# Mixer B's query weights in smaller tiles, a fourth raw weight buffer, other hands for the first down sums, and a later norm

## The chip, the core and the metric

The kernel runs on one core of one Trainium2 chip. What is compared is the device time of one execution in microseconds (us), as the median of several runs. One run of each kernel is also profiled; every duration below comes from that profile or from the runs' times. Engines are named as in the profile: PE (TensorE matmuls), PEld (its weight loads), DVE (VectorE), ACT (ScalarE), POOL (GpSimd), SP (SyncE, which issues transfers here).

## The reference: what is computed

Two layers over 512 positions of width 1024, in float32. The parts that this case touches:

```
for l in range(2):
    h = rms_norm(x, norm_mix[l]);  z = h @ w_in[l]
    qa, ka, va, qi, ki, wi, cq, ckv, kr, ga, gb = split(z)
    # mixer A: index scores relu(qi.ki)*wi -> top 128 keys per query -> sparse attention
    y_a = sparse_indexed_attention(qa, ka, va, qi, ki, wi, rel_bias, 128)
    # mixer B: latent attention
    qb = rope(rms_norm(cq) @ b_w_uq[l])          # 384 -> 8 heads x 96
    k, v = split(rms_norm(ckv) @ b_w_ukv[l])     # 256 -> 8 heads x (64 + 64)
    y_b = latent_attention(rms_norm(qb), rms_norm([k, rope(kr)]), v)
    x = x + (sigmoid(ga)*(y_a @ w_proj_a[l]) + sigmoid(gb)*(y_b @ w_proj_b[l])) @ w_out[l]
    h = rms_norm(x, norm_ffn[l])
    val, gat = split(causal_dwconv(h @ w_up[l]))
    x = x + (silu(gat) * val) @ w_down[l]        # 2816 -> 1024
```

## The kernel before

Activations lie transposed, the 128 partitions holding features and the 512 columns the positions. Every float32 product is made of three matmuls of a narrower kind: each operand is split into a high part and a low part (high times high, high times low, low times high). So each weight tile passes through three stages, all in the class `Weights`: a load from HBM into a raw buffer `wr` (issued on SP, line 154), a cast into the high part `wh` (ACT, L171, or L189 for down tiles), and the low part `wl`. The low part is a DVE subtraction (L183, or L194 for down tiles), or, for the tiles named in `DL` (`gb`, `ga`, `uv`, `ug`, `kv`, `uq`), a negated copy on ACT (L199) onto which a transfer issued by POOL adds the raw tile (L200, "wl<-wr"). There are `WB[0]` = 3 raw buffers and `WB[1]` = 4 buffers each for high and low parts, all as wide as the widest tile, `W_COLS`. A raw buffer is free again when its tile's low part is made. `PLAN` lists the tiles in the order of use; `ahead()` runs at the end of each tile's matmuls, splits the tiles up to three ahead and issues the loads behind them.

A down tile ("dn", 512 loaded columns) is made into seven blocks by three operations (`sums`): L209 and L210 (128x128 subtractions) and L211 (a 128x256 addition). L211 is always on POOL; L210 is on POOL in the second FF part only (`SU2 = '12'`), L209 never.

The program runs: index-query tiles `qi`, index key tile `kiw`, latents `ckv` and `cq`, with the index scores (L319, L320 on PE, `rl` on ACT L983, `sc` on DVE L984) set between them; then mixer B (`kv` L815, `uq` L852, scores L1125 to L1127, softmax) between the `gb` gate tiles, while DVE works off the top-128 search in spare slots (MAX8, L996, and MATCH_REPLACE8, L1003); then mixer A, the merge, and the feed-forward stage in two parts, each with its up tiles `uv`, `ug` and then its down tiles. A helper, `later(n, f)`, puts work on an engine `n` ticks after the point where it is written, one tick per three matmuls; all queues run strictly in the order that results, so a waiting instruction holds everything behind it on its engine.

The norm at the head of a layer adds up squares on DVE (`sq`, L457) and then reduces them with four 1-column matmuls against `ones` (`finish`, L463). `LAG_F` and `LAG_G` say how many ticks later these are put, in layer 0 and in layer 1.

The query weights of mixer B are in one tile of 1152 columns per group of four heads (3 blocks of 384). Its nine matmuls per bank go block by block: high tile twice, low tile once.

## Time and profile before

| | us |
|---|---|
| median of 3 runs (1553.75 to 1557.57) | 1554.92 |
| the profiled execution | 1551.76 |
| its span | 1550.0 |
| PE busy / PEld busy in the span | 1532.2 / 1335.8 |
| DVE / ACT / POOL busy in the span | 1126.9 / 944.7 / 376.9 |

The span is the time between the first and the last instruction of the profiled execution; 1.76 us lie around it. PE's busy time counts matmuls whose ends are modelled, so a matmul behind a wait is shown somewhat long and the idle time ahead of it somewhat short. The granted clock of TensorE was 1.0 of full speed (2.4 GHz) throughout.

### The profile page before, as it was taken

To read this page: it belongs to the slowest core of one execution; us is meant where nothing else is said; L and a number is where in the kernel's file an instruction comes from. 1 tells how busy PE (TensorE), PEld (TensorE's weight loads), DVE (VectorE), ACT (ScalarE), POOL (GpSimd) and SP (SyncE) were. 2 spreads that over 40 slices of the span, in tenths; PEclk is the share of its full clock that TensorE was granted. 3 is DMA by queue.
4 is the path that set the end of the run, shared out by engine and by line. 5 is a ranking of instruction groups with operands and counts; after the bars stand their busy time and mean duration, and the time that the engine had idled before them with its cause. 6 is when DMAs were issued, how large, how long until landed. Compare 5 with 4: busy or idle time off the path is not lost.

```text
span 1550.0 us, 23962 instructions
## 1 busy us (share of the span) xinstructions
PE 1532.2 (99%) x8662; PEld 1335.8 (86%) x8662; DVE 1126.9 (73%) x2323; ACT 944.7 (61%) x1547; POOL 376.9 (24%) x550
## 2 busy tenths in 40 slices
PE   9999999999999999999999999999999999999998
PEld 7887999888888898889988889998888888988898
DVE  7799988666476683548879999886574857835487
ACT  6756677773567535764467576687635764366542
POOL 1233003300012241224602420124001113312254
PEclk9999999999999999999999999999999999999999
DMA  7573134733478437983455721346435883489733
GB/s 249 152 174 96 55 96 98 189 111 134 122 183 198 109 97 196 224 190 84 123 176 121 185 82 55 102 123 168 140 98 137 187 196 89 120 205 211 178 96 103
DMA packets 71687, 219.02 MB, mean 141 GB/s; under 512 B 8384, under 2 KB 8680, under 8 KB 71440
## 3 DMA queue, kind: packets, MB, share of 16 engines
q1 hardware_dynamic: 53248, 149.41, 31.0%
q0 software_dynamic: 17856, 65.28, 23.0%
q10 hardware_dynamic: 464, 2.79, 0.6%
q8 instruction: 68, 1.11, 0.3%
q14 instruction: 51, 0.42, 0.1%
HBM read 143.77 MB, written 6.84 MB: 97 GB/s over the span
## 4 chain that ended last, share of the span: by engine, by line
PE 74%; DVE 10%; DMA 3%; ACT 2%; issue 2%; POOL 1%; DVEq 0%; POOLq 0%; SPq 0%; ACTq 0%
PE D L519 35%; PE T L519 13%; PE D L542 7%; PE L L1381 4%; PE T L1381 3%; PE Y L1041 2%; PE T L1034 2%; PE D L1381 2%; DMA wr<-in_wd_dram 2%; PE Y L1381 2%; DVE wl L194 1%; PE L L519 1%; PE L L320 1%; PE L L319 1%; DMA wl<-wr 1%
## 5 line engine op out<-in xcount | busy, mean ns | idle before, releaser
L171 ACT CAST wh<-wr 128x1024 fp32r<-128x1024 f32 x202 | 211.8, 1050 | 172.6 <-PE D L519 63.2
L200 POOL DMA_DIRECT2D wl<-wr x124 | 107.3, 873 | 640.1 <-ACT wl L199 587.1
L519 PE MATMUL D<-hxh,wh 128*128 128x512 f32 (+1 forms) x448 | 176.8, 395 | 0.9 <-ACT sqc L634 0.9
L519 PE MATMUL D<-hxl,wh 128*128 128x512 f32 (+1 forms) x448 | 175.5, 392 | 0.0
L189 ACT CAST wh<-wr 128x896 fp32r<-128x896 f32 x88 | 82.7, 941 | 118.0 <-POOL wr L211 101.9
L199 ACT ACTIVATE wl<-wr 128x1024 fp32r<-128x1024 f32 x124 | 131.5, 1061 | 33.5 <-PE D L519 21.8
L211 POOL TENSOR_TENSOR wr<-wr 128x256 f32<-128x256 f32 x88 | 101.9, 1158 | 90.9 <-DVE wr L210 77.1
L1076 POOL TENSOR_TENSOR P<-M,sel 128x128 f32<-128x128 f32 (+1 forms) x64 | 54.3, 902 | 277.1 <-DMA M<-skewd 253.0
L519 PE MATMUL D<-hxh,wl 128*128 128x512 f32 (+1 forms) x448 | 120.4, 394 | 0.0
L194 DVE TENSOR_TENSOR wl<-wr,wh 128x896 fp32r<-128x896 f32 x88 | 104.5, 1187 | 13.5 <-ACT wh L189 12.3
L542 PE MATMUL D<-wh,hxh 128*128 128x256 f32 x384 | 114.0, 298 | 0.0
L542 PE MATMUL D<-wl,hxh 128*128 128x256 f32 x384 | 108.8, 284 | 0.0
L542 PE MATMUL D<-wh,hxl 128*128 128x256 f32 x384 | 108.3, 282 | 0.0
L183 DVE TENSOR_TENSOR wl<-wr,wh 128x1024 fp32r<-128x1024 f32 x78 | 97.3, 1251 | 8.2 <-ACT wh L171 6.6
L519 PE MATMUL D<-hrl,wh 128*128 128x512 f32 x256 | 99.6, 389 | 0.0
L519 PE MATMUL D<-hrh,wh 128*128 128x512 f32 x256 | 99.6, 389 | 0.0
L519 PE MATMUL T<-hrh,wh 128*128 128x512 f32 x256 | 99.6, 389 | 0.0
L519 PE MATMUL T<-hrl,wh 128*128 128x512 f32 x256 | 99.6, 389 | 0.0
L519 PEld LDWEIGHTS D<-hxh,wh 128*128 128x128 f32 x448 | 84.4, 188 | 14.3 <-ACT sqc L634 1.3
L519 PEld LDWEIGHTS D<-hxl,wh 128*128 128x128 f32 x448 | 84.4, 188 | 12.6
L519 PEld LDWEIGHTS D<-hxh,wl 128*128 128x128 f32 x448 | 81.1, 188 | 13.3
L299 DVE TENSOR_TENSOR ptl<-T,pth 128x512 fp32r<-128x512 f32 (+3 forms) x128 | 61.0, 485 | 21.4 <-ACT pth L298 20.3
(400 smaller groups left out, 4516.6 us busy)
## 6 DMA issues: line engine op xcount, KB each, us to landing
wr<-in_wd_dram SPq DMA_DIRECT2D x198, 512.0 KB, 3.9
wl<-wr POOLq DMA_DIRECT2D x120, 512.0 KB, 5.5
wr<-in_wd_dram SPq DMA_DIRECT2D x88, 256.0 KB, 2.7
x<-in_xT_dram SPq DMA_DIRECT2D x16, 256.0 KB, 5.1
M<-skewd SPq DMA_DIRECT2D x16, 256.0 KB, 4.0
skewd<-biasd ACTq DMA_DIRECT2D x1, 2560.0 KB, 13.9
wr<-in_wd_dram SPq DMA_DIRECT2D x4, 576.0 KB, 4.2
wl<-wr POOLq DMA_DIRECT2D x4, 576.0 KB, 6.2
```

The costliest lines, as they stand in the source:

```text
L171: ins = self.nc.scalar.copy(h[:, :n], t[:, :n])
L183: eng.tensor_tensor(out=o[:, c], in0=t[:, c], in1=h[:, c].bitcast(F32), op=OP.subtract)
L189: self.nc.scalar.copy(h[:, :896], t[:, 128:1024])
L194: self.later(lag, lambda: self.nc.vector.tensor_tensor(out=o[:, :896], in0=t[:, 128:1024], in1=h[:, :896].bitcast(F32), op=OP.subtract))
L199: self.nc.scalar.activation(o, t, AF.Copy, scale=-1.0)
L200: self.nc.gpsimd.dma_start(o.bitcast(F32), t, accum_op=OP.add)
L211: g(2)(out=b[:, 6:8], in0=b[:, 0:3:2], in1=b[:, 3:6:2], op=OP.add)
L299: later(lag, lambda: V.tensor_tensor(out=o, in0=src, in1=h.bitcast(F32), op=OP.subtract))
L519: mm(p[:, t0:], lhsT=w, rhs=x[:, t0:], start=n == 0, stop=n == len(seq) - 1, skip_group_check=True)
L542: mm(pp[b][:, t, :], lhsT=x, rhs=w, start=n == 0 and half == 0 and t == 0, stop=n == 11 and half == 1, skip_group_check=True)
L1076: G.tensor_tensor(out=P[:, P0[i]:P0[i] + w], in0=M[:, 512 - w:512], in1=sel[:, SEL0[i]:SEL0[i] + w], op=OP.add)
L1381: mm(p, lhsT=w, rhs=x, start=b0, stop=b1, skip_group_check=True)
```

## The change

Three settings and two pieces of code differ. `LAG_F` and `LAG_G` go from 26 to 29 ticks. `WB[0]`, the number of raw buffers, goes from 3 to 4. Each `uq` tile of 1152 columns becomes two, of 768 and 384 columns, so `W_COLS` falls from 1152 to 1024 and all raw, high and low buffers become narrower; the nine matmuls of a bank now take the six products with high parts first and the three with low parts after. And in `sums`, a down tile whose fourth predecessor is not a down tile (the first four of each FF part) has all three operations on POOL.

```diff
-LAG_F = 26
+LAG_F = 29
-WB = [3, 4, 3]
+WB = [4, 4, 3]
-LAG_G = 26
+LAG_G = 29
@@ dense_plan
-    p += [("kv", 0, 1024), ("uq", 0, 1152)]
+    p += [("kv", 0, 1024), ("uq", 0, 768), ("uq", 1, 384)]
-    p += [("kv", 1, 1024), ("uq", 1, 1152)]
+    p += [("kv", 1, 1024), ("uq", 2, 768), ("uq", 3, 384)]
@@ Weights.sums
         su = SU2 if self.seq[i][1] % 11 >= FS // 2 else SUMS
+        if self.seq[i - WB[1]][0] != "dn":
+            su = "012"
@@ attn_b
-            h, o = W.get("uq", g)
+            tiles = [W.get("uq", 2 * g + i) for i in range(2)]
...
-                seq = ([(x, h, k) for k in range(3) for x in xs[k]] + [(xs[k][0], o, k) for k in range(3)] if "k" in LO
-                       else [q for k in range(3) for q in ((xs[k][0], h, k), (xs[k][1], h, k), (xs[k][0], o, k))])
-                for n, (x, w, k) in enumerate(seq):
-                    mm(p[:, 0:384], lhsT=x, rhs=w[:, k * 384:(k + 1) * 384], start=n == 0, stop=n == 8,
-                       skip_group_check=True)
+                seq = [(x, 0, k) for k in range(3) for x in xs[k]] + [(xs[k][0], 1, k) for k in range(3)]
+                for n, (x, part, k) in enumerate(seq):
+                    w = tiles[k // 2][part][:, k % 2 * 384:k % 2 * 384 + 384]
+                    mm(p[:, 0:384], lhsT=x, rhs=w, start=n == 0, stop=n == 8, skip_group_check=True)
@@ lay_out: the host lays the two pieces out one behind the other
```

The lines of the changed kernel below `sums` are one or two higher in number than before (L463 becomes L465, L519 becomes L521, L633 becomes L635).

What this does to the order on the engines, at three places. First, ACT in layer 0, behind the two casts of the index key (`kih`): `ckr` and `sqc` empty the first `ckv` bank of PE, `wn` is the copy from which the index weights are made, `wh` and `wl` belong to the next weight tile. Before:

```order
L571 CAST kih_481<-ki_479 64x512
L171 CAST wh_590<-wr_455 128x1024
L586 COPY wn_501<-T_496 128x160
L199 ACTIVATE wl_591<-wr_455 128x1024
L633 ACTIVATE ckr_528<-D_457,vec 128x512
L634 ACTIVATE sqc_529<-D_457 128x512
L983 ACTIVATE rl_547<-L_544,w_81_503 128x512
```

After:

```order
L573 CAST kih_492<-ki_490 64x512
L635 ACTIVATE ckr_504<-D_459,vec 128x512
L636 ACTIVATE sqc_505<-D_459 128x512
L588 COPY wn_523<-T_518 128x160
L171 CAST wh_574<-wr_396 128x1024
L984 ACTIVATE rl_558<-L_555,w_84_525 128x512
L199 ACTIVATE wl_575<-wr_396 128x1024
```

The two readers of the PE bank moved ahead of the weight tile's cast and copy. Second, PE in layer 1 at the norm's products (`T<-ones,sq`), within the `kiw` tile. Before:

```order
L519 MATMUL L_8483<-hxl_8039,wh_8374 128x512
L463 MATMUL T_8491<-ones,sq_7832 128x1 x4
L519 MATMUL L_8483<-hxh_8044,wh_8374 128x512
L519 MATMUL L_8483<-hxl_8045,wh_8374 128x512
L519 MATMUL L_8483<-hxh_8239,wh_8374 128x512
```

After:

```order
L521 MATMUL L_8499<-hxl_8055,wh_8390 128x512
L521 MATMUL L_8499<-hxh_8060,wh_8390 128x512
L521 MATMUL L_8499<-hxl_8061,wh_8390 128x512
L521 MATMUL L_8499<-hxh_8255,wh_8390 128x512
L521 MATMUL L_8499<-hxl_8256,wh_8390 128x512
L521 MATMUL L_8499<-hxh_8259,wh_8390 128x512
L521 MATMUL L_8499<-hxl_8260,wh_8390 128x512
L521 MATMUL L_8499<-hxh_8328,wh_8390 128x512
L521 MATMUL L_8499<-hxl_8329,wh_8390 128x512
L521 MATMUL L_8499<-hxh_8332,wh_8390 128x512
L465 MATMUL T_8516<-ones,sq_7848 128x1 x4
```

The products stand nine matmuls of 512 columns later (in layer 0 it is two). The index scores, which follow from the norm's result, stand mostly nine to eleven matmuls later in layer 1 as well, and in layer 0 too from the sixth on (the first three keep their place there). Third, POOL at the end of the first part's up tiles in layer 0; tile numbers are printed behind `wl` and `wr`, and the added `uq` tiles make the first down tile number 80 where it was 78. Before:

```order
L200 DMA wl75_5569<-wr75_5477 128x1024
L200 DMA wl76_5607<-wr76_5537 128x1024
L211 TENSOR_TENSOR wr78_5611<-wr78_5611 128x256
L1301 TENSOR_TENSOR t_963_5668<-c_957_5575 128x256
L200 DMA wl77_5643<-wr77_5573 128x1024
L211 TENSOR_TENSOR wr79_5647<-wr79_5647 128x256
```

After:

```order
L200 DMA wl77_5585<-wr77_5457 128x1024
L211 TENSOR_TENSOR wr80_5589<-wr80_5589 128x128
L212 TENSOR_TENSOR wr80_5589<-wr80_5589 128x128
L213 TENSOR_TENSOR wr80_5589<-wr80_5589 128x256
L200 DMA wl78_5623<-wr78_5493 128x1024
L211 TENSOR_TENSOR wr81_5627<-wr81_5627 128x128
L212 TENSOR_TENSOR wr81_5627<-wr81_5627 128x128
L213 TENSOR_TENSOR wr81_5627<-wr81_5627 128x256
L1302 TENSOR_TENSOR t_963_5684<-c_957_5591 128x256
L200 DMA wl79_5659<-wr79_5553 128x1024
```

The first two down tiles' sums moved ahead of the last two up tiles' transfers `wl<-wr` (tiles 78 and 79 now), where one moved operation stood ahead of the last alone.

## Rows read from the trace of the kernel before

**Rows 1.** The page's first two lines: the span, then busy time of each engine.

```profile
span 1550.0 us, 23962 instructions
PE 1532.2 (99%) x8662; PEld 1335.8 (86%) x8662; DVE 1126.9 (73%) x2323; ACT 944.7 (61%) x1547; POOL 376.9 (24%) x550
```

**Rows 2.** Busy time of each engine in six stretches of the span, with the number of instructions, the granted clock, the DMA engines' share and GB/s.

```profile
15.00:60.00 45.00, 43.32 (x216) 36.37 (x215) 32.68 (x59) 32.03 (x52) 8.75 (x20) 1.00 0.62 188
60.00:165.00 105.00, 102.63 (x525) 85.27 (x524) 104.41 (x303) 69.16 (x141) 34.16 (x85) 1.00 0.53 128
525.00:580.00 55.00, 54.90 (x419) 52.93 (x418) 47.71 (x88) 22.30 (x30) 23.17 (x19) 1.00 0.31 87
...
715.00:780.00 65.00, 63.38 (x514) 62.04 (x512) 57.50 (x82) 31.53 (x43) 36.36 (x39) 1.00 0.42 121
780.00:830.00 50.00, 48.78 (x250) 42.98 (x250) 38.30 (x70) 33.30 (x51) 5.71 (x14) 1.00 0.44 139
830.00:935.00 105.00, 103.60 (x534) 86.02 (x533) 104.52 (x304) 70.78 (x143) 34.33 (x85) 1.00 0.54 128
```

**Rows 3.** The chain of work that ended last, one piece within 478 to 490 us: start, length, what.

```profile
480.16 5.45 PE D L519 x24
```

**Rows 4.** PE's timeline in layer 0 at the norm's products and at the first `cq` bank: start, duration, engine, line, operation, out<-in, and in brackets the idle time before and what ended it.

```profile
30.27 1.02 PE L463 MATMUL T<-ones,sq 128*128 128x1 f32 x8 [0.83 <-DVE sq L457]
...
46.83 0.39 PE L320 MATMUL L<-kil,qie 128*128 128x512 f32 x1
48.08 0.50 PE L519 MATMUL D<-hxh,wh 128*128 128x512 f32 x1 [0.85 <-ACT sqc L634]
48.41 0.39 PE L519 MATMUL D<-hxl,wh 128*128 128x512 f32 x1
```

**Rows 5.** ACT's timeline ahead of that second wait.

```profile
43.49 1.05 ACT L171 CAST wh<-wr 128x1024 fp32r<-128x1024 f32 x1 [2.96 <-PE D L519]
...
46.87 0.67 ACT L633 ACTIVATE ckr<-D,vec 128x512 f32<-128x512 f32 x1
47.44 0.59 ACT L634 ACTIVATE sqc<-D 128x512 f32<-128x512 f32 x1
```

**Rows 6.** PE's timeline: matmuls that waited around the boundary of the layers, and near the end of the first FF part of layer 1.

```profile
766.36 0.38 PE L1381 MATMUL D<-b11h,wl 128*128 128x256 f32 x1 [0.73 <-DVE wl L194]
...
772.70 0.39 PE L1381 MATMUL D<-b11h,wh 128*128 128x256 f32 x1 [0.21 <-ACT wh L189]
...
779.29 0.44 PE L325 MATMUL L<-hxh,wl 128*128 128x384 f32 x1 [0.56 <-DVE wl L183]
...
799.02 1.02 PE L463 MATMUL T<-ones,sq 128*128 128x1 f32 x8 [0.79 <-DVE sq L457]
...
1352.26 0.38 PE L1381 MATMUL L<-b11h,wl 128*128 128x256 f32 x1 [0.49 <-DVE wl L194]
```

**Rows 7.** The way of down tiles through the engines before the layer boundary: DVE's, POOL's and ACT's timelines.

```profile
766.43 1.08 DVE L194 TENSOR_TENSOR wl<-wr,wh 128x896 fp32r<-128x896 f32 x1
769.18 0.29 DVE L209 TENSOR_TENSOR wr<-wr 128x128 f32<-128x128 f32 x1 [1.68 <-DMA wr<-in_wd_dram]
...
772.02 0.29 DVE L209 TENSOR_TENSOR wr<-wr 128x128 f32<-128x128 f32 x1 [0.61 <-DMA wr<-in_wd_dram]
...
772.89 1.08 DVE L194 TENSOR_TENSOR wl<-wr,wh 128x896 fp32r<-128x896 f32 x1
...
769.61 0.46 POOL L210 TENSOR_TENSOR wr<-wr 128x128 f32<-128x128 f32 x1 [0.97 <-ACT wh L189]
770.15 1.52 POOL L211 TENSOR_TENSOR wr<-wr 128x256 f32<-128x256 f32 x1
...
771.71 0.94 ACT L189 CAST wh<-wr 128x896 fp32r<-128x896 f32 x1 [1.82 <-POOL wr L211]
```

**Rows 8.** DVE's and POOL's timelines where both run at once: a `wl` subtraction of the same shape as in [rows 7], and a sum.

```profile
764.68 1.62 DVE L194 TENSOR_TENSOR wl<-wr,wh 128x896 fp32r<-128x896 f32 x1
...
764.29 1.07 POOL L211 TENSOR_TENSOR wr<-wr 128x256 f32<-128x256 f32 x1
```

**Rows 9.** The first down tile of layer 0 on DVE, and POOL's transfers for the last two up tiles (tiles 76 and 77).

```profile
515.98 0.29 DVE L209 TENSOR_TENSOR wr<-wr 128x128 f32<-128x128 f32 x1 [8.30 <-DMA wr<-in_wd_dram]
...
508.75 0.86 POOL L200 DMA_DIRECT2D wl<-wr  x1 [4.58 <-ACT wl L199]
...
518.65 0.87 POOL L200 DMA_DIRECT2D wl<-wr  x1
```

**Rows 10.** From the page's list of DMA issues: KB each, median us to landing.

```profile
wl<-wr POOLq DMA_DIRECT2D x120, 512.0 KB, 5.5
```

**Rows 11.** PE's timeline in mixer B: three of its waits.

```profile
113.25 0.50 PE L815 MATMUL L<-wh,ckvh 128*128 128x512 f32 x1 [0.55 <-DVE vb L299]
...
135.83 0.50 PE L1125 MATMUL L<-tbh,tbh 100*128 100x512 f32 x1 [1.04 <-ACT P L353]
...
905.85 0.33 PE L1034 MATMUL T<-ident,P 128*128 128x128 f32 x1 [0.25 <-DVE P L1023]
```

**Rows 12.** One step of the top-128 search on DVE.

```profile
830.35 0.69 DVE L996 MAX8 m<-sc 128x8 f32<-128x512 f32 x1
```

**Rows 13.** DVE's timeline ahead of the wait at 1352 us.

```profile
1346.06 0.29 DVE L209 TENSOR_TENSOR wr<-wr 128x128 f32<-128x128 f32 x1 [1.21 <-DMA wr<-in_wd_dram]
...
1351.12 1.08 DVE L194 TENSOR_TENSOR wl<-wr,wh 128x896 fp32r<-128x896 f32 x1
```

More of the change, by code (lines that the diff above doesn't have):

```diff
@@ L1483, in tile_of @@
         if name == "uq":
-            return tiles_t(a["b_w_uq"][l][:, 384 * idx:384 * (idx + 1)])
+            w = a["b_w_uq"][l][:, 384 * (idx // 2):384 * (idx // 2 + 1)]
+            return tiles_t(w[256:] if idx % 2 else w[:256])
         o = {"qi": O_QI, "ckv": O_CKV, "cq": O_CQ, "ga": O_GA, "gb": O_GB}.get(name)
```

## The prediction, made before the changed kernel was run

> **What bounds the kernel now.** I read the page's busy times first [rows 1]. PE is busy for 1532.2 of 1550.0 us, so at most 17.8 us of it can be idle, and no edit here takes a matmul away: the same matmuls are only ordered otherwise. That PE's busy time is honest is seen in the chain [rows 3]: 24 matmuls of 512 columns take 5.45 us, 0.227 us each, end on end. So the change can win only what PE waits for, and the stretches [rows 2] say where that is: idle 1.68 us in 15 to 60, 2.37 in 60 to 165 (mixer B of layer 0), 0.10 in 525 to 580, 1.62 in 715 to 780 (last down tiles of layer 0), 1.22 in 780 to 830 and 1.40 in 830 to 935 (mixer B of layer 1). Most of the rest lies at the start and in the tail, which nothing here touches. In the two mixer B stretches DVE is busy 104.41 and 104.52 of 105 us: there DVE is the bound, and PE's waits follow DVE.
>
> A printed wait costs more than its brackets. At 46.83, 48.08 and 48.41 [rows 4] two matmuls take 1.58 us instead of 0.45, so a wait printed as 0.85 costs 1.1. I add 0.27 to each printed wait of an ordinary matmul.
>
> **The change, part by part.**
>
> *Norm, layer 0.* The products wait 0.83 us for the last sum of squares [rows 4]. They now stand two matmuls later: 2 x 0.227 = 0.45 us of that wait is filled with other work. -0.45.
>
> *The `cq` bank at 48 us.* PE waits because ACT empties `D` late: `ckr` and `sqc` (46.87 to 48.03) stand behind a cast that itself began at 43.49 after waiting 2.96 us for PE, and a copy that waits too [rows 5]. In the new order both stand right behind the `kih` casts, ahead of that cast. They need only that `ckv` bank, which PE had filled before the 24 matmuls (5.45 us [rows 3]) of the bank behind it, and those end ahead of 46.83. The wait goes: -1.1. Together -1.55 us by the time mixer B of layer 0 begins.
>
> *Raw buffers, layer boundary.* The fourth buffer's use shows in [rows 7]. A down tile's load can be issued only when the low part three tiles back is done: DVE's subtraction at 766.43 is followed by 1.68 us of idle until the next tile lands, and then sum, POOL's 0.46 and 1.52, ACT's 0.94, DVE's 1.08, done at 773.97. From the end of the low part at 766.3 that is 7.7 us for three tiles, 2.6 per tile; PE uses one in 21 x 0.12 = 2.5 us (an estimate from 256-column matmuls at half the 0.227). With four buffers the same loop gives 7.7 / 4 = 1.9. So the waits of [rows 6] at 766.36 and 772.70 go: 0.73 + 0.21 + 2 x 0.27 = 1.5 us, and 0.4 for one at 775.6 that is too short to be printed. At 779.29 (0.56, and a shorter one behind it) the low part of a `qi` tile is late after DVE has been without a gap from 772; DVE gains the 1.68 + 0.61 us of idle, but PE arrives 1.9 earlier as well, so I count 0.4 of it. Sum -2.3. Bounds: 0 if DVE's queue and not the load sets it, -3.3 if the `qi` waits go too.
>
> *Norm, layer 1.* Nine matmuls later is 2.04 us, more than the wait of 0.79 [rows 6]; the 1-column matmuls refill in 0.1. -0.9.
>
> *Raw buffers, 1352 us.* DVE idles 1.21 us at 1346.06 for a late tile, and the subtraction PE waits for stands seven operations behind, with no gap left [rows 13]. The wait of 0.49 + 0.27 goes: -0.75.
>
> *First four tiles' sums on POOL.* 24 subtractions of 0.29 us leave DVE. In the first part of layer 0 they matter least at once: DVE sat idle 8.30 us before the first of them, holding everything behind it [rows 9]. That is worth something 20 us later, where 525 to 580 has 0.10 us of PE idle in it: -0.3 (bounds 0 and -0.5). What POOL now does ahead of the last two up tiles' transfers: it waits for a landing and runs 0.46 + 0.46 + 0.73 us. The transfer for tile 76, issued at 508.75, then comes about 2 us later. It lands 5.5 us after issue [rows 10], so near 516.5. When PE needs it is bounded by the next one: tile 77's transfer went out at 518.65, landed near 524, and made PE wait for nothing that shows (0.10 us of idle in 525 to 580); tile 76 is used one tile, 5.45 us, sooner, so it may land at 518.7 at least. Tile 77's own transfer stays near its old place, since the second down tile's load also lands one tile sooner. Cost 0 while the delay stays under some 2 us; bound +0.5 at each of four ends of up stretches. SP has one more load in its queue ahead of the `xd` stores, for which nobody waits soon.
>
> *Query tiles in two.* Eight more casts and copies on ACT and four more transfers on POOL (0.86 each), both far from full in the stretch (69.16 and 34.16 of 105) [rows 2]; PE's matmuls are as many. High products first leaves the low part more time. 0, bounds -0.3 (a wait on the low part that I don't see) and +0.5 (ACT's in-order wait for a free `wh` buffer holding a softmax step).
>
> *What mixer B gives back.* This is the open term. PE comes to it 1.55 us earlier in layer 0 and 2.3 + 0.9 = 3.2 earlier in layer 1. But DVE's full stretch begins with the index scores, and these stand nine to eleven matmuls, 2.0 to 2.5 us, later in PE's order. So in layer 1 DVE starts about 3.2 - 2.1 = 1.1 us earlier, and in layer 0 between 1 us earlier (its first scores keep their place) and 0.7 later. From then on DVE has no slack, and where PE waits for it, PE's gain is cut to DVE's. Against that the search steps stand elsewhere: counted in DVE's order, three fewer steps stand ahead of `vb` and `qn` of layer 0 (about 1.4 us at 0.69 for a 512-column step [rows 12] and less for the narrower), two more ahead of its first softmax sum (+0.9), and six more there in layer 1 (+2.8), where PE's order also has 2 to 3 us more work put ahead. So the waits at `vb` (113.25) shrink or stay, and the one at 135.83, printed as 1.04, stays [rows 11]. I take +0.35 back in layer 0 (net -1.2; bounds -2.2 and 0) and +1.75 in layer 1 (net -1.45; bounds -3.3 and +0.5).
>
> **Sum.** -1.2 - 0.3 - 1.45 - 0.75 = -3.7 us on the profiled 1551.76, so 1548.1. The profiled run lies 3.2 us under the median of the runs shown, so I take the 3.7 off the median: 1551.2 us.
>
> **A rule against it.** The row first: the same `wl` subtraction takes 1.08 us alone [rows 7] and 1.62 while POOL runs a sum [rows 8], so a sum that leaves DVE for POOL can cost DVE up to 0.54 us elsewhere, against 0.29 saved. The Trainium skill, Perfetto Trace Analysis, section Optimizing Scalar/DVE Operations, says that the two engines share an SBUF read port, so that moving work between them "might not help". The trace agrees with it as to the stretching. By that rule the term for the sums is 0 or a loss; by my reading of the idle 8.30 us it is -0.3. As a mechanism of this kernel it is rival 4.
>
> **Rivals.**
> 1. *DVE follows.* The search steps moved back let DVE reach its results in time and nothing is given back: -1.55 - 0.3 - 3.2 - 0.75 = -5.8, 1549.1 us. For it: waits at `vb` and `qn` have 1.4 us less ahead of them in layer 0. Against it: DVE's 104.5 of 105.
> 2. *Mixer B takes everything.* DVE ends both stretches no sooner than before: only -0.3 - 0.75 remain, 1553.9 us. For it: the index scores' later place. It is also what comes out if the load was not what held the boundary.
> 3. *Slower: DVE's full stretch begins later.* If the boundary is bound by DVE's queue (the bound 0 above), then in layer 1 the index scores come 2.0 - 0.9 = 1.1 us later than before, in layer 0 0.7 later, and the search steps put ahead of the softmax (0.9 and 2.8) come on top where PE has nothing to fill in: +5.5 - 0.75 = +4.8, 1559.7 us. It decides once DVE's first search step stands more than 0.9 us later than before in both layers. Against it: the idle of 1.68 us in [rows 7] is named as a DMA's.
> 4. *POOL and DVE disturb each other.* Four `wl` subtractions per part stretched by 0.54 are 2.2 us of DVE, less 4 to 8 x 0.29 saved. In the first parts, where PE's wait in 525 to 580 shows DVE close, PE would wait about 1 us in each layer: -3.7 + 2.0 = -1.7, 1553.2 us.
>
> **How the numbers follow.** Chances: forecast 0.35, rival 1 0.27, rival 2 0.18, rival 3 0.10, rival 4 0.10. A measurement of this kernel can tell about 0.3%, 4.7 us, from no change. Rival 1 and the better quarter of the forecast are beyond that (0.27 + 0.09, with some of the bounds: 0.38); rival 3 is the slower side, 0.10; the rest, 0.52, is within it. The range from 1546.5 (every term at its better bound, -8) to 1557.0 (rival 2 with a mishap of the size of a run's spread) leaves out rival 3 and a little on either side. The forecast alone: 1549 to 1553.
>
> **What would show it.** Right: no PE wait at 48 us nor ahead of `ones` in layer 1; no DVE idle for `wr` between 750 and 775; PE idle in the stretch 715 to 780 under 0.5; DVE's wait of 8.30 us at the first down tile gone and a like one on POOL; PE idle in the stretch 830 to 935 larger than 1.40, as DVE holds PE. Wrong: the boundary waits still there with the loads early (DVE's queue was it), or idle in 830 to 935 as small as before with the whole 3.2 us kept (rival 1).

## The result, and the profile of the changed kernel

The changed kernel takes 1544.96 us (median, 1544.32 to 1545.92) where the kernel before, beside it, took 1555.45 (1553.75 to 1557.77): a ratio of 0.9933, with an interval from 0.9921 to 0.9945. In a second measurement, in the third of the four sets below, it took 1545.70 against 1555.76, a ratio of 0.9939 (0.9922 to 0.9956). It is faster by about 10 us both times. (In the other three sets, where the changed kernel was not run, the kernel before took 1553.1 to 1553.3.) The prediction had 1551.2 us and a range that ended at 1546.5, so it was wrong, by 6.2 us. One run of one kernel below, "all but sums", took 3068 us, twice the others, and is in none of the figures.

The profiled execution took 1544.84 us, that of before 1551.76: the two traces differ by 6.9 us, which is 3.2 more than the forecast 3.7. The other 3 us of the miss lie between the traces and the medians: the profiled execution of before was 3 to 4 us quicker than its median, that of the changed kernel equals its own.

The page of the changed kernel begins so (as in [rows 1]):

```profile
span 1543.1 us, 23959 instructions
PE 1530.5 (99%) x8662; PEld 1337.7 (87%) x8662; DVE 1121.6 (73%) x2299; ACT 948.0 (61%) x1555; POOL 391.7 (25%) x578
```

PE is idle for 12.6 us instead of 17.8. DVE has lost 24 instructions and 5.3 us, POOL has gained 28 and 14.8 us. The six stretches of [rows 2] in the changed kernel, with the same columns:

```profile
15.00:60.00 45.00, 45.00 (x224) 37.97 (x223) 32.35 (x60) 32.71 (x54) 9.89 (x22) 1.00 0.65 204
60.00:165.00 105.00, 103.15 (x526) 85.58 (x526) 103.76 (x301) 68.98 (x144) 35.43 (x86) 1.00 0.52 127
525.00:580.00 55.00, 55.00 (x428) 53.60 (x427) 49.65 (x85) 24.39 (x31) 18.47 (x17) 1.00 0.36 101
715.00:780.00 65.00, 65.00 (x529) 64.76 (x528) 58.20 (x88) 33.10 (x46) 34.10 (x36) 1.00 0.47 146
780.00:830.00 50.00, 49.68 (x255) 43.35 (x254) 37.82 (x78) 33.97 (x56) 6.58 (x15) 1.00 0.43 126
830.00:935.00 105.00, 103.97 (x557) 88.15 (x556) 104.57 (x306) 69.24 (x145) 35.49 (x86) 1.00 0.53 127
```

Idle time of PE is gone altogether in three of them (1.68, 0.10 and 1.62 us before). In the last row, mixer B of layer 1, PE's idle time went down from 1.40 to 1.03 us, though DVE is as full as before. The eight largest waits of PE over the whole span (engine, line, what it waited for: us in total, times, longest):

```profile
PE T L374 <- DVE warm L370: 1.2, 1, 1.2
PE L L817 <- DVE vb L301: 1.1, 2, 0.7
PE L L325 <- ACT wh L300: 1.0, 2, 0.6
PE T L1111 <- DVE qao L315: 0.5, 2, 0.2
PE T L1035 <- DVE P L1024: 0.4, 1, 0.4
PE L L1126 <- ACT P L355: 0.4, 1, 0.4
PE T L1035 <- DVE kal L765: 0.4, 2, 0.2
PE L L321 <- ACT rl L984: 0.3, 1, 0.3
```

The waits of [rows 4] and [rows 6] for `sq`, for `sqc` and for a down or `qi` tile's `wl` are all missing from it. The last row is new: in layer 1, at 815.62 us, a product of the index scores waits for `rl`.

I followed the lead, that is how much earlier the same matmul starts in the changed kernel than before, through the trace of before and two traces of the changed kernel; the second is that of "once more" below. These are differences of start times, worked out matmul by matmul (minus is a gain):

| Stretch | Forecast | Measured | Second trace |
|---|---|---|---|
| Start, to 16 us | 0 | +0.81 (clock, below) | -0.16 |
| Norm of layer 0 and `cq` bank, to 81 us | -1.55 | -1.95 | -1.40 |
| Mixer B, layer 0 | +0.35 | +0.49 | -0.05 |
| The middle of layer 0, at 283 us | 0 | -0.59 | -0.74 |
| 545 us (the sums) | -0.3 | -0.50 | -0.54 |
| Layer boundary, 760 to 790 us | -2.3 | -3.42 | -3.64 |
| Norm of layer 1, to 850 us | -0.9 | -0.34 | -0.26 |
| Mixer B, layer 1 | +1.75 | -0.87 | -0.89 |
| 960 to 1150 us (mixer A) | 0 | -0.04 | +1.53 |
| 1352 us | -0.75 | -0.74 | -0.74 |
| End of the span | -3.7 | -6.9 | -6.7 |

(Small shifts between the stretches make up the difference to the sum.) The largest miss is mixer B of layer 1, by 2.6 us, and its sign is wrong. The boundary brings 1.1 to 1.3 us more than forecast, and the norm of layer 1 some 0.6 less: it wins 1.0 us at 799 us, as it should, and about 0.6 of that goes to the new wait for `rl`. In the first trace PE comes 0.81 us late to the norm of layer 0, so its wait for `sq` is gone altogether; in the second PE comes in time and a wait of 0.37 us is left at 30 us, as the forecast of -0.45 for this wait has it (0.83 before).

### The profile page after: what moved, and what is told of

Its sections match the earlier page's. It is cut to its first block, busy times and chain, and to the rows that moved or that the text cites. A ratio compares the mean times of both kernels' runs of the same rounds, so it can differ in the third digit from the quotient of the medians.

```text
span 1543.1 us, 23959 instructions
## 1 busy us (share of the span) xinstructions
PE 1530.5 (99%) x8662; PEld 1337.7 (87%) x8662; DVE 1121.6 (73%) x2299; ACT 948.0 (61%) x1555; POOL 391.7 (25%) x578
## 4 chain that ended last, share of the span: by engine, by line
PE 81%; DVE 8%; ACT 2%; issue 1%; DMA 0%; POOL 0%; SPq 0%; ACTq 0%; DVEq 0%
PE D L521 35%; PE T L521 15%; PE D L544 7%; PE L L1382 5%; PE T L1382 4%; PE D L1382 3%; PE Y L1042 2%; PE Y L1382 2%; PE T L1035 2%; PE L L521 2%; DVE sc L1004 1%; DVE m L997 1%; PE L L322 1%; PE L L321 1%; DVE mx L1129 1%
## 5 line engine op out<-in xcount | busy, mean ns | idle before, releaser
L171 ACT CAST wh<-wr 128x1024 fp32r<-128x1024 f32 (+1 forms) x206 | 212.4, 1034 | 160.0 <-PE D L521 66.9
L200 POOL DMA_DIRECT2D wl<-wr x128 | 111.0, 880 | 631.1 <-ACT wl L199 599.8
L521 PE MATMUL D<-hxh,wh 128*128 128x512 f32 (+1 forms) x448 | 176.5, 394 | 0.0
L521 PE MATMUL D<-hxl,wh 128*128 128x512 f32 (+1 forms) x448 | 175.2, 391 | 0.0
L199 ACT ACTIVATE wl<-wr 128x1024 fp32r<-128x1024 f32 (+2 forms) x128 | 132.1, 1035 | 47.2 <-PE D L521 25.1
L521 PE MATMUL D<-hxh,wl 128*128 128x512 f32 (+1 forms) x448 | 119.2, 393 | 0.0
L213 POOL TENSOR_TENSOR wr<-wr 128x256 f32<-128x256 f32 x88 | 94.2, 1073 | 62.4 <-DVE wr L212 49.2
L194 DVE TENSOR_TENSOR wl<-wr,wh 128x896 fp32r<-128x896 f32 x88 | 101.8, 1159 | 6.9 <-ACT wh L189 2.9
L521 PE MATMUL D<-hrl,wh 128*128 128x512 f32 x256 | 99.6, 389 | 0.0
L521 PE MATMUL D<-hrh,wh 128*128 128x512 f32 x256 | 99.6, 389 | 0.0
L521 PE MATMUL T<-hrh,wh 128*128 128x512 f32 x256 | 99.6, 389 | 0.0
L521 PE MATMUL T<-hrl,wh 128*128 128x512 f32 x256 | 99.6, 389 | 0.0
L521 PEld LDWEIGHTS D<-hxh,wh 128*128 128x128 f32 x448 | 84.4, 188 | 13.5 <-DVE gb L685 0.2
L521 PEld LDWEIGHTS D<-hxl,wh 128*128 128x128 f32 x448 | 84.4, 188 | 12.7
L521 PEld LDWEIGHTS D<-hxh,wl 128*128 128x128 f32 x448 | 81.4, 188 | 13.8
L1328 DVE SCALAR_TENSOR_TENSOR c<-T,vec,c 128x511 f32<-128x511 f32 x32 | 23.9, 747 | 89.2 <-ACT c L1325 89.2
```

Of the source, the lines that this page charges most:

```text
L171: ins = self.nc.scalar.copy(h[:, :n], t[:, :n])
L194: self.later(lag, lambda: self.nc.vector.tensor_tensor(out=o[:, :896], in0=t[:, 128:1024], in1=h[:, :896].bitcast(F32), op=OP.subtract))
L199: self.nc.scalar.activation(o, t, AF.Copy, scale=-1.0)
L200: self.nc.gpsimd.dma_start(o.bitcast(F32), t, accum_op=OP.add)
L213: g(2)(out=b[:, 6:8], in0=b[:, 0:3:2], in1=b[:, 3:6:2], op=OP.add)
L521: mm(p[:, t0:], lhsT=w, rhs=x[:, t0:], start=n == 0, stop=n == len(seq) - 1, skip_group_check=True)
```

## Experiments

They ran in four sets, each with the kernel before beside it on the same chip (medians 1553.09, 1553.32, 1555.76 and 1553.19 us). "Lead" is told against the trace of before where the text does not name the changed kernel. The first eight take the parts apart:

| Kernel | Lags | Tiles in two | 4th raw buffer | Sums on POOL | us | Ratio to before (interval) |
|---|---|---|---|---|---|---|
| before again | | | | | 1553.56 | 1.0006 (0.9993 to 1.0018) |
| tiles alone | | x | | | 1555.01 | 1.0015 (1.0004 to 1.0025) |
| buffer and tiles | | x | x | | 1557.59 | 1.0028 (1.0016 to 1.0041) |
| lags alone | x | | | | 1550.74 | 0.9979 (0.9968 to 0.9990) |
| sums alone | | | | x | 1553.05 | 0.9993 (0.9983 to 1.0003) |
| all but lags | | x | x | x | 1548.41 | 0.9966 (0.9954 to 0.9977) |
| all but sums | x | x | x | | 1555.12 | 1.0013 (1.0000 to 1.0026) |
| all but the buffer | x | x | | x | 1549.06 | 0.9972 (0.9960 to 0.9983) |

A fourth buffer with whole query tiles was not run.

**The kernel before, once more**, unchanged.

> The kernel before, unchanged, for a second trace. The six unprofiled runs of before have a median 3.7 us above the one execution whose trace was read (1555.45 against 1551.76), while the changed kernel's trace lies on its own median. Theory A, late loads: the waits for raw buffers differ from execution to execution, so this trace is longer by up to 3.7 us with the excess in 500 to 800 and 1300 to 1355 us. Theory B, the start: the excess lies in the first 17 us, with a granted clock under 1.0 there, as in the changed kernel's trace. Theory C: the trace is again near 1551.8 and the excess is spread or not in the span. The time against before is the same in all three (ratio 1.000).

The median is the same. Its trace shows why one trace isn't the kernel: it loses 2.15 us to the trace of before by 61 us and nothing behind that. So theory A does not hold for it, and theory B for 0.84 us alone, lost ahead of 16 us; 1.3 us are lost between 30 and 40 us. The stretch 32 to 40 us in this execution, with the columns of [rows 2] (the granted clock is the last but two):

```profile
32.00:40.00 8.00, 8.00 (x32) 6.38 (x32) 4.25 (x17) 1.78 (x3) 0.00 (x0) 0.80 0.90 293
```

The same stretch in the trace of before:

```profile
32.00:40.00 8.00, 8.00 (x39) 6.62 (x38) 4.47 (x15) 3.88 (x6) 0.00 (x0) 1.00 0.98 313
```

At 0.80 PE starts 32 matmuls in the 8 us instead of 39: a part of the stretch runs at the lower of its two levels, 1.2 instead of 2.4 GHz, right behind the norm's wait at 30 us.

**The query tiles in two, alone.**

```diff
-    p += [("kv", 0, 1024), ("uq", 0, 1152)]
+    p += [("kv", 0, 1024), ("uq", 0, 768), ("uq", 1, 384)]
```

> Only the query tiles in two, with their new order of products; three raw buffers, lags and sums as before. Theory of the forecast: no gain, 0 (-0.3 to +0.5 us). Rival, that the split itself changes the order around mixer B and the first banks: -1 to -2.5 us, with the wait at 48 us for the cq bank gone.

It costs 1.9 us, a loss that neither theory had. PE's timeline in mixer B of layer 1 has a wait that the kernel before doesn't have there, and ACT's timeline another, just ahead of it:

```profile
909.54 1.04 ACT L171 CAST wh<-wr 128x1024 fp32r<-128x1024 f32 x1 [2.56 <-DMA wr<-in_wd_dram]
...
911.58 0.50 PE L1040 MATMUL Y<-pth,vb 128*128 128x512 f32 x1 [1.84 <-ACT pth L298]
```

ACT's cast of a weight tile stands still for 2.56 us because the tile has not landed, and the softmax copy `pth`, for which PE waits, stands behind it in ACT's order: it begins at 910.95 us, before at 907.48. Mixer B of layer 1 takes 2.0 us more in this trace. The prediction's bound of +0.5 had ACT holding a softmax step too, but for a free `wh` buffer, where it is a late load. Of the other traces only one has such a stop of ACT in a mixer B, of 1.21 us at 139 us, that of everything but the fourth buffer, which also has tiles in two and three raw buffers. The wait for `sqc` at 48 us stays in this kernel, and goes with the lags below.

**The fourth raw buffer, with the tiles in two that make room for it.**

```diff
-WB = [3, 4, 3]
+WB = [4, 4, 3]
```

> The split and the fourth raw buffer (which does not fit without the split); lags and sums as before. If the waits of the down tiles are the loads': the PE waits at 766 to 780 and at 1352 us vanish, 3.0 + 0.75 us in the traces, and more in the runs if the loads' lateness varies: -4 to -7 us. If DVE's queue sets them: under -1.5 us.

Slower by 4.5 us, where both theories had a gain, and 2.6 slower than the tiles alone. The waits for down tiles at the layer boundary and at 1352 us are gone (one of 0.34 us for a `qi` tile stays, at 782.31), but PE has new ones in both layers 11 to 14 us into the down products (at 546.75, 547.95, 732.75, 1316.00 and 1317.21 us), all for low parts of activations from DVE.

**The norm's products later, alone.**

```diff
-LAG_F = 26
-LAG_G = 26
+LAG_F = 29
+LAG_G = 29
```

> Only the two lags, 26 to 29. Forecast: the wait ahead of the norm's products shrinks by 0.45 in layer 0 and goes in layer 1 (0.9), -1.35 us before mixer B, of which mixer B gives back most: -0.5 (0 to -1.4). Rival, that the lag also moves the index scores and so the whole order of mixer B to the better: -2 to -3.5 us, with the waits of PE in 830 to 935 us smaller than 1.4.

2.35 us less. No wait for `sqc`, and 1.3 us of lead won between 16 and 66 us, against the forecast of 1.55. Mixer B of layer 1 took 0.13 us more than before, where the forecast was 1.75.

**The sums on POOL, alone.**

```diff
         su = SU2 if self.seq[i][1] % 11 >= FS // 2 else SUMS
+        if self.seq[i - WB[1]][0] != "dn":
+            su = "012"
```

> Only the first four down tiles' sums on GpSimd. Forecast: -0.3 us (0 to -0.5), the wait at 545 us gone. Rival, shared port: DVE's subtractions are stretched beside the sums and PE waits about 1 us more in each first part: +1 to +2 us.

Not to be told from nothing, as forecast (-0.3). PE has no idle time left between 525 and 580 us. The mean of the 88 `wl` subtractions of [rows 8] rises in it from 1187 to 1228 ns, so the stretching of rival 4 is there, 3.6 us of DVE in all, about half of the 24 x 0.29 us that it is spared, and it doesn't reach PE. In the changed kernel the mean is 1159 ns. The rule that the prediction cites (the Trainium skill, Perfetto Trace Analysis, section Optimizing Scalar/DVE Operations) agrees with this trace as to the stretching; what it says of the gain does not hold beside the fourth buffer, as the kernel without the sums shows below.

**Everything but the lags.**

```diff
-LAG_F = 29
-LAG_G = 29
+LAG_F = 26
+LAG_G = 26
```

> The changed kernel with both lags back at 26. If the lags are worth 1.35 us by their waits alone: +1.35 us against the changed kernel, 1546.3. If they carry the order of mixer B in layer 1 as well: +2 to +3.5 us, 1547 to 1548.5. If nothing: 1545.

About 3 us of the changed kernel's gain go. The norm's waits and the one for `sqc` are back, and its trace has a granted clock of 0.66 between 32 and 40 us. Mixer B of layer 1 takes 0.24 us more than before, where it gains 0.87 in the changed kernel.

**Everything but the sums.**

```diff
-        if self.seq[i - WB[1]][0] != "dn":
-            su = "012"
```

> The changed kernel with the sums where they were. By the forecast +0.3 us (1545.3), as DVE's wait at the first down tile is taken away by the earlier load anyway. By the rival in which DVE's block at the head of each down stretch counts once PE has less slack: +1 to +2.5 us.

The whole gain is gone: 1555.12 us. Without the fourth buffer the sums on POOL are worth 0.3 us, and no more beside the lags (0.9980 with both, below, 0.9979 with the lags alone); with it they are worth about 10 (9.7 by the spans of the traces, 1552.8 and 1543.1, and 9.4 to 10.2 by the medians, taken on other chips). Rows of DVE's and PE's timelines in this kernel:

```profile
507.31 0.29 DVE L209 TENSOR_TENSOR wr<-wr 128x128 f32<-128x128 f32 x1 [3.82 <-DMA wr<-in_wd_dram]
...
518.79 0.29 DVE L209 TENSOR_TENSOR wr<-wr 128x128 f32<-128x128 f32 x1 [6.56 <-DMA wr<-in_wd_dram]
...
543.12 0.42 DVE L299 TENSOR_TENSOR b11l<-c,b11h 128x256 fp32r<-128x256 f32 x1
...
544.06 0.69 DVE L299 TENSOR_TENSOR t1l<-t,t1h 128x512 fp32r<-128x512 f32 x1
...
543.60 0.39 PE L1380 MATMUL D<-b11l,wh 128*128 128x256 f32 x1 [0.61 <-DVE b11l L299]
544.80 0.39 PE L1380 MATMUL D<-t1l,wh 128*128 128x256 f32 x1 [0.70 <-DVE t1l L299]
```

DVE takes its work in order. Its sum of a down tile stands early in that order, and DVE stands still until the tile's load has landed: here twice, 3.82 and 6.56 us, 10.4 us in all. In the trace of before it stood still once, 8.30 us [rows 9], in the second trace of the same kernel twice, 4.61 and 4.18 us. Over the six traces with three raw buffers and these sums on DVE it is 8.1 to 9.2 us here in five, and 10.9 in that of the lags alone, which also has the two waits of PE (0.40 and 0.70 us, at 543.50 and 544.71). So the fourth buffer does not bring the standing still, it makes it longer: 11.2 us in the kernel with buffer and tiles. Everything behind waits, among it `b11l` and `t1l`: DVE makes them at 543.12 and 544.06 us, no sooner than before (543.24 and 544.18), though PE comes 1.8 us sooner and finds them late. In the changed kernel they come at 541.51 and 542.45.

In layer 1 the same two matmuls wait 1.43 and 0.70 us at 1311.18 and 1312.39, and what follows costs more than the waits. The stretch from 1312 to 1316 us, with the columns of [rows 2]:

```profile
1312.00:1316.00 4.00, 3.61 (x16) 3.52 (x17) 2.54 (x6) 0.84 (x1) 3.81 (x2) 0.50 0.35 115
```

The granted clock is 0.50 in it and 0.66 in the 4 us behind, so 3.4 us of the 5.5 that this trace loses here to the changed kernel's are the clock's, whose level fell behind the wait. The runs of this kernel go with the clock: at a mean of 0.998 and 0.999 they take 1551.9 to 1555.1 us, at 0.995 and 0.996 they take 1557.3 to 1559.7.

In the changed kernel POOL does this standing, and nothing that PE needs soon is behind it:

```profile
508.50 0.46 POOL L211 TENSOR_TENSOR wr<-wr 128x128 f32<-128x128 f32 x1 [5.56 <-DMA wr<-in_wd_dram]
...
510.25 0.87 POOL L200 DMA_DIRECT2D wl<-wr  x1
...
513.62 0.86 POOL L200 DMA_DIRECT2D wl<-wr  x1
...
519.52 0.52 POOL L211 TENSOR_TENSOR wr<-wr 128x128 f32<-128x128 f32 x1 [5.04 <-DMA wr<-in_wd_dram]
```

The two transfers between them are those of [rows 9] (508.75 and 518.65 before): one goes out 1.5 us later, the other 5 us sooner.

**Everything but the fourth buffer.**

```diff
-WB = [4, 4, 3]
+WB = [3, 4, 3]
```

> The changed kernel with three raw buffers. If the loads set the waits at the layer boundary: +3.8 us in the trace, and up to +7 in the runs if three buffers also make the executions differ by several us as those of before do: 1549 to 1552, with the waits at 766 to 780 and 1352 us back. If DVE's queue set them: under +1.5 us.

The waits of [rows 6] at the boundary are back in PE's timeline, so the buffer is what takes them away:

```profile
764.87 0.38 PE L1382 MATMUL D<-b11h,wl 128*128 128x256 f32 x1 [0.87 <-DVE wl L194]
777.34 0.44 PE L327 MATMUL L<-hxh,wl 128*128 128x384 f32 x1 [0.57 <-DVE wl L183]
778.48 0.44 PE L327 MATMUL L<-hxh,wl 128*128 128x384 f32 x1 [0.34 <-DVE wl L183]
```

By the traces the buffer brings 3.1 us (spans 1546.2 and 1543.1); by the medians 3.4 to 4.1 (1549.06 against 1544.96 and 1545.70). The sum of the forecast was nearly that, 2.3 + 0.75, but its parts are not: the boundary alone is worth 3.1 here, and the wait at 1352 us, expected back with three buffers, stays away. It is missing too from the other kernels with three buffers and the layer-0 products later, and in those with the products at 26 it varies (0.49 and 0.20 us in the two traces of before). So the buffer is not what takes it away in the changed kernel, and what does stays open. Mixer B of layer 1 gains 0.9 us in this kernel too, so the buffer is not what turned it.

**The changed kernel, once more**, on the chip of the next three.

> The changed kernel once more, as it is, beside the same runs of the kernel before as the other kernels of this set. If the first ratio of 0.993 holds: about 1545 us, 8 to 9 us under the kernel before (whose medians elsewhere were 1553.1 and 1553.3), with runs within 2 us of each other and the granted clock of the stretch 32 to 40 us at 1.00. If a part of the first difference was the chip that the kernel before ran on: 1547 us or a difference of under 7 us.

1545.70 us, 1544.39 to 1546.63: the gain holds.

**Only the layer-0 products later; only the layer-1 products later.** `LAG_F = 29` alone, and `LAG_G = 29` alone, in the kernel before.

> Kernel before with only the norm's products of layer 0 put three steps later (layer 1 as before). Theory 'clock': the wait near 30 us lets the granted clock fall in some executions, and that is the larger part of what the later products are worth; then this part alone brings the whole of the 2.35 us that both had brought, about 1550.8, with no run above 1553.5 where the kernel before has some at 1555 to 1559. Theory 'length': it brings just the waits that go, 1.4 us by the trace, 1551.8, and the runs spread over 5 us or more as before.

> Kernel before with only the norm's products of layer 1 put three steps later (layer 0 as before). Theory 'clock': within 1 us of the kernel before, between 1552.5 and 1553.5, since the waits at the end of layer 0 and in mixer B of layer 1 take its 0.9 us back, and with the same wide spread of runs up to 1557 or more. Theory 'length': 0.9 us less, 1552.3, the spread the same too, so that the two kernels with one late norm add up to the one with both only by the second theory.

1553.67 us (0.9986, 0.9972 to 1.0000) and 1553.71 us (0.9990, 0.9979 to 1.0002): 2.1 us each by the medians, with intervals that reach to nothing, so this pair doesn't tell the theories apart by its times. By the traces it tells something. With the layer-0 products late the granted clock is 1.00 from 26 to 60 us; without, in the second of the two, it is 0.81 between 32 and 40. But theory "clock" expected no run above 1553.5 us in the first, and its runs reach 1555.98, so the clock behind 30 us is not the whole of the spread.

**More warming matmuls at the start**, `WARM = 14` in the changed kernel.

> Changed kernel with 14 instead of 10 warming matmuls at the start. In its trace PE idles for 1.15 us between 5 and 8 us and the granted clock is 0.57 from 8 to 12 us, where the kernel before has 0.23 idle and 1.00. If the idle time behind the warming matmuls is what lets the clock fall there, the gap closes, the clock stays at 1.00 to 17 us and the time is 1 to 1.5 us less, 1543.6. If the first weights' landing sets the start anyway: the same 1545, and the clock between 8 and 17 us falls in it too.

In its trace PE's gap between 5 and 8 us closes (busy 3.00 of 3.00) and the granted clock stays at 1.00 to 17 us, as the first theory had it. The span is 1543.1 us all the same, and the median 1546.93 (1544.30 to 1549.85): no gain. The first useful matmul begins at 6.66 us in it, at 5.92 and 5.62 in the two traces of the changed kernel, so the longer warming delays what it is to speed up.

**POOL with the sums of one pair only.** GpSimd takes the first two down tiles of each part in one kernel, the third and fourth in the other.

```diff
-        if self.seq[i - WB[1]][0] != "dn":
+        nth = 0
+        while self.seq[i - nth - 1][0] == "dn":
+            nth += 1
+        if nth in (0, 1):          # (2, 3) in the second kernel
             su = "012"
```

> Changed kernel, but GpSimd takes all sums of only the first two down tiles of each part, and VectorE has its sums of the third and fourth back. Theory 'held': without the sums on GpSimd VectorE stood still twice, 3.8 us at the first pair and 6.6 us at the second; here one hold of about 6 us remains, at the second pair, close to where the activations' low parts are wanted, and the time is 1546 to 1548, up to 2 us over the changed kernel. Theory 'load': half of the 9 to 11 us come back, 1550 to 1551.

> Changed kernel, but GpSimd takes all sums of only the third and fourth down tiles, and VectorE has those of the first two back. Theory 'held': one hold of 4 to 6 us remains, at the first pair, earlier than the one of the kernel before and with 25 us to make it up, so the time is within 1 us of the changed kernel, 1545 to 1546. Theory 'load': half comes back, 1550 to 1551, as with the other pair.

With the second pair on DVE: 1554.64 us, ratio 1.0005 (0.9996 to 1.0015). With the first pair on DVE: 1546.13 us, 0.9958 (0.9945 to 0.9970), nearly as good as the changed kernel. As many subtractions are moved in one as in the other, and the two times lie 8.5 us apart, so theory "load" falls. Theory "held" is right for the first pair and too mild for the second: the hold there costs the whole gain. DVE's holds and PE's waits with the second pair on DVE:

```profile
517.29 0.29 DVE L214 TENSOR_TENSOR wr<-wr 128x128 f32<-128x128 f32 x1 [8.35 <-DMA wr<-in_wd_dram]
...
1283.46 0.29 DVE L214 TENSOR_TENSOR wr<-wr 128x128 f32<-128x128 f32 x1 [9.71 <-DMA wr<-in_wd_dram]
...
1309.03 0.39 PE L1385 MATMUL D<-b11l,wh 128*128 128x256 f32 x1 [1.22 <-DVE b11l L304]
1310.23 0.43 PE L1385 MATMUL D<-t1l,wh 128*128 128x256 f32 x1 [0.70 <-DVE t1l L304]
```

and with the first pair on DVE:

```profile
508.83 0.29 DVE L214 TENSOR_TENSOR wr<-wr 128x128 f32<-128x128 f32 x1 [4.83 <-DMA wr<-in_wd_dram]
```

The hold at the first pair ends at 509, the one at the second at 517, some 26 us ahead of the matmul that wants `b11l`, and DVE needs most of such a time: in 1284 to 1309 us it is busy for 21.38 of 25. In the trace shown the second hold costs 0.6 us at 544, 0.9 at 730, 0.5 at 780 and 4.1 at 1309. Of the 4.1 some 1.7 are the clock's, granted at 0.80 from 1308 to 1312 us and at 0.77 in the 4 us behind. That trace is the quickest execution of that kernel (1551.06); what the others lose beyond it, I can't show.

**The layer-1 products three steps later still**, `LAG_G = 32` in the changed kernel.

> Changed kernel with the norm's products of layer 1 three more steps later. If it is the order that lets VectorE reach the needed results first, mixer B of layer 1 keeps or adds to what it gained: within 0.5 us of the changed kernel or up to 1 us faster. If a later start of the index scores holds VectorE's full stretch, as the prediction had it: slower, by up to 2 us, with new waits of PE between 830 and 935 us.

1547.34 us: slower than the changed kernel by about 2. Against the changed kernel it loses 1.8 us in mixer B, between 849 and 945 us, with three waits for `vb` in the place of one; against the kernel before it loses 0.9 there. PE's waits from 820 to 945 us:

```profile
PE L L817 <- DVE vb L301: 0.8, 2, 0.6
PE L L854 <- DVE vb L301: 0.5, 1, 0.5
PE L L1126 <- ACT P L355: 0.4, 1, 0.4
```

So the prediction's mechanism exists, but three steps further on than it was put, and at half the size (forecast 1.75).

**The lags and the sums alone**, with whole query tiles and three buffers.

> Kernel before with the norm's products three steps later in both layers and the first four tiles' sums on GpSimd, but the query tiles whole and three raw buffers. Its time beside the changed kernel with three raw buffers (0.9972 of the kernel before) prices the query tiles in two under the new order. If the lags alone turn mixer B of layer 1 to a gain: PE's lead grows by 0.5 us or more there and the time is that of the kernel with three buffers, 0.997. If the tiles in two do: no gain there (as with the lags alone, where PE lost 0.1) and 0.998.

1550.01 us, 0.998 (0.997 to 0.999). Mixer B of layer 1 takes 1.0 us more than in the changed kernel, so about as much as before, as with the lags alone. The tiles in two make the difference there, while alone they cost 1.9 us. What they are worth in the whole time under the later products is not settled: 1 us by the medians, on two chips, with ratios (0.998 against 0.9972 without the fourth buffer) whose intervals overlap.

## Why the prediction was wrong, point by point

**What held.** The norm and the `cq` bank: 1.95 us against 1.55 in one trace, 1.40 in the other, and the `sqc` wait goes with the lags and with no other part. The layer boundary is held by the load and not by DVE's queue: with three buffers the waits for down tiles are there, with four they are not, in every pairing. (A wait of 0.34 to 0.35 us for a `qi` tile stays with four in the three kernels where DVE has the sums of the third and fourth tiles.) The transfer for tile 76 on POOL: 1.5 us later, at no cost. One of the signs was put wrongly: DVE's idle time for a `wr` at the boundary did not go, it stands at another place where nothing hangs on it:

```profile
764.76 0.67 DVE L211 TENSOR_TENSOR wr<-wr 128x128 f32<-128x128 f32 x1 [1.61 <-DMA wr<-in_wd_dram]
```

**What came out by luck.** At the layer boundary and the norm behind it the forecast was 3.2 us and 3.8 came, but by two misses that offset: the boundary brought 3.4 us for 2.3, above the bound of 3.3, because the waits for `qi` tiles went too, and the norm of layer 1 kept 0.3 us of 0.9, because the index scores found `rl` late. At 1352 us 0.74 came for 0.75, but the wait is gone with three buffers as well, so the reason given, the buffer, is not the one at work.

**The step that failed in the sum: "What mixer B gives back", layer 1.** It read DVE's 104.5 of 105 us as a bound on PE, started DVE's full stretch at the index scores, put these 2.1 us later against a PE that came 3.2 earlier, and counted six search steps ahead of the softmax as delay. Four groups of DVE, from 820 to 960 us in the kernel before (line, count: least/median/greatest ns, first and last start) and then in the changed one:

```profile
L996 DVE MAX8 m<-sc x48: 402/548/695, 828.8 to 940.5; 128x8 f32<-128x512 f32 x16, 128x8 f32<-128x384 f32 x16, 128x8 f32<-128x256 f32 x16
...
L299 DVE TENSOR_TENSOR vb<-L,vb x8: 407/411/416, 868.2 to 887.3; 128x256 fp32r<-128x256 f32 x8
...
L884 DVE TENSOR_TENSOR qn<-qn,y x8: 529/546/551, 888.0 to 912.9; 128x384 f32<-128x384 f32 x8
...
L1007 DVE TENSOR_SCALAR sel<-sc x3: 260/352/415, 946.3 to 947.0; 128x512 bf16<-128x512 f32 x1, 128x384 bf16<-128x384 f32 x1, 128x256 bf16<-128x256 f32 x1
```

```profile
L997 DVE MAX8 m<-sc x48: 405/546/695, 822.5 to 934.6; 128x8 f32<-128x512 f32 x16, 128x8 f32<-128x384 f32 x16, 128x8 f32<-128x256 f32 x16
...
L301 DVE TENSOR_TENSOR vb<-L,vb x8: 403/408/413, 862.4 to 881.5; 128x256 fp32r<-128x256 f32 x8
...
L885 DVE TENSOR_TENSOR qn<-qn,y x8: 527/546/567, 882.2 to 909.8; 128x384 f32<-128x384 f32 x8
...
L1008 DVE TENSOR_SCALAR sel<-sc x3: 278/327/415, 940.5 to 942.9; 128x512 bf16<-128x512 f32 x1, 128x384 bf16<-128x384 f32 x1, 128x256 bf16<-128x256 f32 x1
```

The search begins 6.3 us earlier, not 1.1: it waits for the first scores alone, and the scores put later fall among its steps. `vb`, for which PE waits, and the first `qn` come 5.8 us earlier, the whole of PE's lead (5.5 us at 850); the last `qn` comes 3.1 earlier. The end of the search, the last selection, is only 4.1 us earlier: search steps were put behind what PE needs, and the search stretches by 2.2 us (from 118.2 to 120.4). So a DVE that is busy all the time had work in it that could be put off. This is rival 1, "DVE follows" (-5.8 us; the traces say -6.9), which the prediction had at 0.27 and argued against with "DVE's 104.5 of 105". Its sign came true as well: PE's idle time in 830 to 935 us fell, to 1.03. How much can be put off is bounded: three steps more cost 2 us. And it takes two parts. The later products alone only break even there (0.12 and 0.13 us lost, in the two kernels with whole tiles), the tiles in two alone lose (0.24 to 2.0 us in three kernels), and with both mixer B gains 0.87 to 1.02 us in all seven traces that have them at 29. The prediction had the tiles at 0. With whole tiles and the later products PE waits 0.59 us for a `qn`, at 888.69 and 885.91 us, and with tiles in two it does not; why it does not I did not take apart further.

**The step that failed in the base: 3.7 us "off the median".** The sum was made against the profiled execution, and the prediction took the gap of 3.2 us between it and the median for something that stays. It doesn't: the changed kernel's runs lie within 2.3 us of each other, those of before over 7 to 10 us in each of the four sets. The larger cause is the clock, and the record has it for every run: of the 103 runs of the kernel before in the four sets, the 12 with a mean granted clock of 1.000 took 1551.4 us in the mean, the 26 at 0.999 1553.0, the 35 at 0.998 1554.0 and the 30 at 0.997 1556.1. The trace of before has 1.000, so the forecast was made on one of the few executions that lost nothing. The changed kernel's twelve runs all have 0.998 or 0.999 (1545.6 and 1545.2 us). One place where the clock is lost is seen. With the layer-0 products at 26, six of seven traces have PE's wait at 30 us (0.50 to 0.84 us), and in four of these six the granted clock between 32 and 40 us is 0.66 to 0.83; with the products at 29, where that wait is 0.37 us at most, it is 1.00 in all eleven traces. A granted clock of 0.66 to 0.83 over 8 us is 1.4 to 2.7 us lost in such an execution. So the norm's wait was worth more than its length, in executions that the one trace did not show. It is not the only such place: the kernel with only the layer-0 products late has runs up to 1556 us, at 0.998 and 0.999. Nor is the clock the whole of the spread. The trace with only the layer-1 products late has a wait of 1.40 us for a `ptl` at 1053 us, that of the lags alone one of 0.65 for the same, and no other has it there, which points to lateness in DVE that varies from run to run. The changed kernel is not free of such things: its second trace loses 1.53 us between 960 and 1150 us. Why its runs still lie so close together is not shown.

**A term mis-sized: the sums, -0.3.** That is what they are worth alone (0.9993), and the prediction priced them alone. But the fourth buffer makes DVE stand still longer for them (10.4 to 11.2 us where it was 8 to 9 as a rule), so that beside it they are worth about 10 us, a good third of it in the trace by the clock that fell behind PE's wait. The prediction saw the 8.30 us of [rows 9] and didn't ask what a fourth load would make of them. Its sum came out near the right mechanism only because both parts are in the change: had it been asked of the buffer alone, it would have said -3 us, and the chip says +2.6.

The slower rival was not at work, nor was rival 2: the leads at the boundary and in mixer B are both kept. Rival 4's stretching is real and small.

## What to carry to other kernels

Another prefetch buffer can lengthen the time for which work stands waiting for a landing: look in which engine's order that work stands and what is behind it, and give it to an engine whose queue can stand still. A full engine is a bound only for the results that others wait for; see which of its work can be put off before counting its busy share as a wall. And where runs of the kernel spread over more than the difference asked for, a single trace is the base for the terms of a sum, not for what a wait is worth in the usual run.

## What the runs showed of the hardware that I had not expected

A wait of TensorE of 0.50 to 0.84 us at 30 us was followed by a stretch with a granted clock of 0.66 to 0.83 in four executions, so that a part of it ran at the lower level, 1.2 GHz; in two others, with waits of 0.81 and 0.83 us, the clock stayed at 1.00. Two waits close together at 1309 to 1317 us, of 1.17 to 1.43 and 0.70 us, were followed by 0.50 to 0.80 over 4 us in all three executions that have them, while two such waits at 544 to 548 us left the clock at 1.00 in one of the three, the kernel with buffer and tiles. The start shows the same variation: 0.57 in the stretch 8 to 12 us in one trace of the changed kernel, 1.00 in the other, behind idle times of 1.15 and 0.32 us between 5 and 8 us. The idle time does not decide it: 1.16 us left the clock at 1.00 in the kernel without the sums, and 0.69 was followed by 0.64 with the tiles alone. The Trainium skill, TensorE: Matmul & The Clock Gate, Part 1: The HAM clock gate, says that the chip's monitor of TensorE's activity runs freely, so that the same kernel differs from execution to execution at its start. The starts of these traces agree with it; none of them shows the monitor itself.
